# Two-layer attention trunk on one core: the general bias body, the rotary product and the casts of weight slices rewritten

## The chip, the cores and the metric

The kernel runs on one core of a Trainium2 chip. The metric is the device time of one execution in microseconds, the median of several runs. Engines are named as in the profile: PE is TensorE (matrix products; PEld its weight loads), DVE is VectorE, ACT is ScalarE, POOL is GpSimd, and SP is SyncE, which only issues transfers. ACT issues transfers too. Names with a q (ACTq, SPq) are an engine's instruction queue.

## What is computed

The input is x with 1024 rows of width 1024, and one integer position for each row. Two layers follow each other, each `h <- h + rmsnorm(mixer(rmsnorm(h)))`.

Layer A projects u = rmsnorm(x) to queries, keys, values and a gate (16 heads of 64). A row attends to its own chunk of 64 rows and the 8 chunks before. A learned bias per head is added to the scores, taken by the difference of positions clipped to -128..128:

```python
rel = jnp.clip(qpos[:, :, None] - kpos[:, None, :], -MAX_REL, MAX_REL) + MAX_REL
bias = jnp.take(rel_bias, rel, axis=1).transpose(1, 0, 2, 3)
```

After layer A one shared set of keys and values is projected from the residual stream. Layer B is differential attention on it: 8 heads with two softmax maps each, the second one subtracted with a learned factor, block-causal. Its queries and the shared keys get a rotary embedding on the first 16 of each 64 columns:

```python
return jnp.concatenate([t1 * cos - t2 * sin, t2 * cos + t1 * sin, t[..., ROT_DIM:]], axis=-1)
```

## The kernel before

All products are made in float32 in three passes: an operand is cut into a rounded part hi and a remainder lo (`hi_of`, line 188, a cast on ACT; `lo_of`, line 191, a subtraction on DVE), and hi·hi, hi·lo and lo·hi are added up (`mm_group`, line 264, lines 269, 271 and 273). A projection group is 24 matmuls into one of two accumulators, 512 rows at a time.

The order is written out by hand in ticks (class `Ticks`). In a tick PE issues four steps of the stream of dense products (`program`, line 1053), and each other piece of work is entered for a tick: `K.at` puts it ahead of the four, `K.after` and `K.later` behind them, `later(k)` k ticks from now, in the order of a rank and then of entry. Every engine works its own instructions strictly in the order in which they were issued. The stream is: 64 projection groups of layer A (head pairs u = 0 to 7; kinds key, query, value, gate; two halves of the rows), the output product of A, 64 groups of layer B, the output product of B. Attention steps of pair u are entered 24 ticks after its first group, one block of 128 rows every six ticks (`attA`, `attB`).

**The start.** Small loads, x tiles and the first weights are issued; ACT makes the square sums of x tiles 0 and 1 (`x_rstd`, line 355, its unused squares go to a slot of R2); PE makes 22 warm-up transposes. A flag tells whether the positions are not consecutive. It is read into a register of every engine (line 400), and `tc.If` (line 401) runs `general_bias` (line 1094), which builds the bias tiles for arbitrary positions. With the inputs here the flag is 0 and the body is jumped over. It holds 134 transfers on SP, unrolled over four groups of heads and eight row tiles, and inner loops. The pool `late` (line 404) is opened behind it and lies over its space; R1 and R2, which hold the operands of the dense products, lie elsewhere from the first. Then `norm_in` (line 475) normalises tile by tile (square sum on ACT, scale on POOL, line 480 on DVE), PE transposes (line 165), and ACT and DVE cut the result into R1.

**The bias.** For consecutive positions the bias tile of a head is the same for all rows. `bias_build` (line 441) makes it from a skewed copy of the table: `part1` loads it, `part2`, seven ticks later, fills its constant columns on DVE and stores it to slot 8 of the head's tensor `bias_t[h]`. `attA_pair` loads a tile for each block six ticks ahead of the scores, by an index that the flag selects (lines 635 to 637). `scores` (line 602) adds it on DVE and takes the maximum. The scores `sp` have a single buffer.

**Weight slices.** A's slices of 128x1024 are cut whole by `w_split` (line 199). B's are prepared during A (`Prepared.prepare`, line 230): loaded on ACT's queue, scaled on POOL (line 244), cut whole (`cut`, line 236), and stored by SP to `wcut` three ticks after the cast.

**The turn to layer B.** `layer_b_tiles` (line 869), six ticks ahead of B's first group, clears the cosine and sine tables, the mask and two buffers `sw` on POOL and loads the tables with eight transfers on SP.

**Rotation.** Each key or query group of B goes through `rope` (line 884). ACT copies the accumulator to `xs` (line 893); SP moves four strips of 8 rows into `sw` with rows swapped (lines 895, 896); DVE makes `xc`, the accumulator times the cosine (line 899); POOL multiplies `sw` by the sine (line 901) three ticks after the group; DVE adds both (line 902) six ticks after it, five for pair 0. A tick later ACT and DVE cut the sum into R1 (`split_k`, line 530, `split_q`, line 513); for a query, two transfers on SP (line 520, `R<-R`) copy the cut rows to the other half of the partitions. `xs`, `xc`, the values' copy `vt` and the gate's `th` share a ring of three buffers. In `attB_block` (line 922), `close` scales an output on DVE (line 1000) by a factor that POOL computes (lines 178, 179).

## Time and profile before

| | |
|---|---|
| median of 3 runs | 1328.13 us (1327.79 to 1331.78) |
| the profiled execution | 1329.67 us, span 1327.8 us |
| PE busy | 1290.0 us, 97% |
| DVE, ACT, POOL busy | 826.2, 685.1, 450.2 us |
| mean granted clock of PE | 0.99 |

The span runs from the first instruction to the last; the rest of an execution's time lies around it. A busy engine is not always one that sets the end: what counts is which engine waits for which, and when.

### The profile page before, as it was taken

The page shows a single profiled execution, that of the slowest core. Times are in us where ns is not written, and L with a number is a line of the kernel's source. Part 1 is how long each engine was busy: PE and PEld are TensorE (multiplying, and loading weights), DVE is VectorE, ACT ScalarE, POOL GpSimd, SP SyncE. Part 2 cuts the span into 40 slices and gives each one's busy share as a digit, 9 for nine tenths or more (in the row PEclk, how much of TensorE's full clock was granted, in tenths as well). Part 3 has the DMA queues.
Part 4 walks back from the last instruction along what each step waited for, and adds up shares of the span by engine and source line. Part 5 has one row for each costly group of instructions (what it writes and reads, how often), then busy time and mean ns, then how long its engine had stood idle before and what let it go on. Part 6 is the DMA issues. An engine that isn't in the chain of part 4 may idle for free.

```text
span 1327.8 us, 20645 instructions
## 1 busy us (share of the span) xinstructions
PE 1290.0 (97%) x6919; PEld 1090.8 (82%) x6919; DVE 826.2 (62%) x1719; ACT 685.1 (52%) x1488; POOL 450.2 (34%) x688
## 2 busy tenths in 40 slices
PE   6899999999999999999997999999999999999997
PEld 5788888888888888888886888888888888888786
DVE  5466665656575656665434676757575758588643
ACT  5456575656565656654333454545454545456311
POOL 1146444555545454442221222212121212122321
PEclk8999999999999999999998999999999999999999
DMA  5477767776677778655443232323232323225343
GB/s 215 117 259 226 229 216 233 242 233 231 229 251 246 236 223 268 205 176 151 148 134 115 77 107 73 107 76 108 75 109 74 109 74 109 74 78 172 99 151 107
DMA packets 103094, 211.24 MB, mean 159 GB/s; under 512 B 14432, under 2 KB 49280, under 8 KB 102976
## 3 DMA queue, kind: packets, MB, share of 16 engines
q1 hardware_dynamic: 80448, 135.85, 32.7%
q10 hardware_dynamic: 22528, 73.95, 17.2%
q8 instruction: 57, 0.93, 0.3%
q14 instruction: 61, 0.50, 0.1%
HBM read 135.19 MB, written 58.83 MB: 146 GB/s over the span
## 4 chain that ended last, share of the span: by engine, by line
PE 80%; issue 5%; POOL 5%; DVE 3%; ACT 2%; DMA 2%; SPq 1%; ACTq 0%; POOLq 0%; DVEq 0%
PE acc L269 15%; PE acc L271 14%; PE acc L273 14%; PE acc L782 12%; PE sp L597 8%; PE tp L165 8%; PE av L981 4%; PE av L699 4%; POOL st L169 1%; POOL s L651 1%; DVE R L192 1%; POOL w L244 1%; DMA skew<-rev 1%; ACT R L189 1%; DMA sw<-xs 0%
## 5 line engine op out<-in xcount | busy, mean ns | idle before, releaser
L273 PE MATMUL acc<-R,wlo 128*128 128x512 f32 x1008 | 410.4, 407 | 0.0
L269 PE MATMUL acc<-R,whi 128*128 128x512 f32 x1008 | 405.4, 402 | 0.7 <-DVE xc L899 0.7
L271 PE MATMUL acc<-R,whi 128*128 128x512 f32 x1008 | 404.7, 401 | 0.1
L612 ACT ACTIVATE s<-s,st 128x640 f32<-128x640 f32 (+7 forms) x256 | 188.2, 735 | 135.1 <-DVE st L606 131.5
L192 DVE TENSOR_TENSOR R<-tp,R 128x512 fp32r<-128x512 f32 (+3 forms) x304 | 178.8, 602 | 85.3 <-ACT R L189 83.9
L169 POOL TENSOR_TENSOR st<-st,mone 128x1 f32<-128x1 f32 x192 | 128.2, 668 | 277.5 <-ACT s L612 254.9
L273 PEld LDWEIGHTS acc<-R,wlo 128*128 128x128 f32 x1008 | 191.1, 190 | 33.0
L271 PEld LDWEIGHTS acc<-R,whi 128*128 128x128 f32 x1008 | 191.4, 190 | 30.8 <-DVE R L192 0.4
L269 PEld LDWEIGHTS acc<-R,whi 128*128 128x128 f32 x1008 | 191.7, 190 | 29.0 <-DVE xc L899 1.1
L189 ACT CAST R<-tp 128x512 fp32r<-128x512 f32 (+3 forms) x304 | 155.3, 515 | 107.6 <-PE tp L165 104.3
L597 PE MATMUL sp<-R 128*128 128x256 f32 (+3 forms) x768 | 174.3, 335 | 10.5 <-DVE st L606 6.3
L606 DVE CUSTOM_DVE_ANT_0 s<-sp,mask 128x256 f32<-128x256 f32 (+7 forms) x128 | 96.6, 755 | 111.3 <-PE sp L597 111.2
L597 PEld LDWEIGHTS sp<-R 128*128 128x128 f32 x768 | 136.4, 189 | 32.4 <-DVE st L606 8.1
L782 PE MATMUL acc<-R,ohi 128*128 128x512 f32 x512 | 161.0, 394 | 0.0
L606 DVE CUSTOM_DVE_ANT_0 s<-sp,bt 128x640 f32<-128x640 f32 (+4 forms) x128 | 83.7, 654 | 75.0 <-PE sp L597 50.0
L165 PEld LDWEIGHTS tp<-ident,s 128*128 128x128 f32 x768 | 96.0, 140 | 39.1 <-DVE s L950 10.6
L165 PE MATMUL tp<-ident,s 128*128 128x128 f32 x768 | 124.1, 274 | 0.9 <-DVE s L950 0.8
L901 POOL TENSOR_TENSOR sw<-sw,sin 128x512 f32<-128x512 f32 x32 | 43.0, 1344 | 225.0 <-DMA sw<-xs 203.9
L782 PEld LDWEIGHTS acc<-R,ohi 128*128 128x128 f32 x512 | 94.7, 188 | 18.5
L178 POOL TENSOR_SCALAR st<-st 128x1 f32<-128x1 f32 x80 | 20.7, 259 | 242.7 <-ACT tt L185 190.0
L782 PE MATMUL acc<-R,olo 128*128 128x512 f32 x256 | 101.5, 397 | 0.0
L651 POOL TENSOR_SCALAR s<-s,st 128x640 f32<-128x640 f32 (+4 forms) x128 | 90.7, 708 | 12.6
(123 smaller groups left out, 1639.2 us busy)
## 6 DMA issues: line engine op xcount, KB each, us to landing
bt<-bias_t SPq DMA_DIRECT2D x64, 320.0 KB
R<-R SPq DMA_DIRECT2D x64, 256.0 KB
wcut<-wh SPq DMA_DIRECT2D x32, 512.0 KB
wcut<-w SPq DMA_DIRECT2D x32, 512.0 KB
whi<-wcut ACTq DMA_DIRECT2D x32, 512.0 KB
wlo<-wcut ACTq DMA_DIRECT2D x32, 512.0 KB
wst<-in_a_w_in_dram ACTq DMA_DIRECT2D x29, 512.0 KB
w<-in_kv_w_dram ACTq DMA_DIRECT2D x16, 512.0 KB
```

The costliest lines, as they stand in the source:

```text
L165: T.transpose(dst, src, ident)
L169: G.tensor_tensor(out=r, in0=a, in1=mone, op=ALU.pow)
L189: A.copy(out=hi, in_=src)
L192: V.tensor_tensor(out=lo, in0=src, in1=hi.bitcast(F32), op=ALU.subtract)
L269: T.matmul(acc, lhsT=hi[:, c, :], rhs=xT(0, c), start=(c == 0), stop=False)
L271: T.matmul(acc, lhsT=hi[:, c, :], rhs=xT(1, c), start=False, stop=False)
L273: T.matmul(acc, lhsT=lo[:, c, :], rhs=xT(0, c), start=False, stop=(c == NC - 1))
L597: T.matmul(sp[:, a:b], lhsT=q[:, l, (i % 4) * P:(i % 4 + 1) * P], rhs=ks[:, head, j0 * P + a - c0:j0 * P + b - c0], start=(l == 0), stop=( ...
L606: V.tensor_tensor_reduce(out=s[:, 0:w], in0=sp, in1=add, op0=ALU.add, op1=ALU.min, scale=-0.125, scalar=BIG, accum_out=mx)
L612: A.activation(s[:, 0:w], s[:, 0:w], AF.Exp, bias=mx, scale=-1.0, accum_out=sums)
L651: G.tensor_scalar(out=s[:, 0:w], in0=s[:, 0:w], scalar1=r, scalar2=0.5, op0=ALU.mult, op1=ALU.mult)
L782: T.matmul(y, lhsT=lhs[:, c, :], rhs=R[:, n * 8 + c, l * 512:(l + 1) * 512], start=(m == 0), stop=(m == 23))
```

## The change

It has seven parts.

- `tc.If` gets `preferred_fallthrough_block=False`: the compiler is asked to place the code that follows when the flag is 0 right behind the branch.
- `general_bias` becomes a loop over the row tiles with all 16 heads at once and four transfers, on ACT's queue instead of SP's. For that the 16 tensors `bias_t[h]` become one tensor with the head as its first index.
- R1 and R2 move to a pool `resident` that is opened behind the general body and lies over its space; the pool `late` is opened ahead of it. The unused squares go to a tile `squares` in one of late's three `bb` buffers.
- `w_split` and `cut` cut a slice in two halves, a tick apart, and the store to `wcut` comes four ticks after the first cast instead of three.
- `part2` of the first two heads' bias comes four ticks after `part1` instead of seven.
- `layer_b_tiles` comes 40 ticks ahead of layer B instead of six.
- In `rope` the product with the cosine is made on POOL, in place in `xs`, two ticks after the group; DVE no longer reads the accumulator, and `xc` is gone. The sum is made six ticks after the group for pair 0 too, and in pair 0 the scores of blocks 0 and 1 are entered one tick later.

```diff
-    bias_t = [dp.tile([NT + 1, P, 640], F32, name=f"bias_t{h}") for h in range(AH)]
+    bias_t = dp.tile([AH, NT + 1, P, 640], F32, name="bias_t")
...
         hi, lo = w_tile("whi"), w_tile("wlo")
-        K.later(0, lambda: hi_of(w, hi), 2)
-        K.later(1, lambda: lo_of(w, hi, lo), 2)
+        for k in range(2):
+            c = slice(k * 4, k * 4 + 4)
+            K.later(k, lambda c=c: hi_of(w[:, c, :], hi[:, c, :]), 2)
+            K.later(k + 1, lambda c=c: lo_of(w[:, c, :], hi[:, c, :], lo[:, c, :]), 2)
...
-                K.later(0, lambda: hi_of(w, hi.bitcast(F32R)))
-                K.later(1, lambda: lo_of(w, hi.bitcast(F32R), w.bitcast(F32R)), 2)
-                K.later(3, lambda: [dma(out=wcut[k][:, 0, :], in_=hi), dma(out=wcut[k][:, 1, :], in_=w)])
+                for j in range(2):
+                    c = slice(j * 512, j * 512 + 512)
+                    K.later(j, lambda c=c: hi_of(w[:, c], hi[:, c].bitcast(F32R)), 2)
+                    K.later(j + 1, lambda c=c: lo_of(w[:, c], hi[:, c].bitcast(F32R), w[:, c].bitcast(F32R)), 2)
+                K.later(4, lambda: [dma(out=wcut[k][:, 0, :], in_=hi), dma(out=wcut[k][:, 1, :], in_=w)])
...
+    squares = lp.tile([P, D], F32, tag="bb", name="squares", bufs=3)
+
     def x_rstd(t):
-        return rstd_of([sumsq(xts[t], R2[:, 10 + t % 2, :])], D)
+        return rstd_of([sumsq(xts[t], squares)], D)
...
-    with tc.tile_pool(name="general", bufs=1) as gp, tc.If(flag > 0):
+
+    with tc.tile_pool(name="general", bufs=1) as gp, tc.If(flag > 0, preferred_fallthrough_block=False):
         general_bias(nc, tc, gp, positions, rel, bias_t)
-
-    lp = ctx.enter_context(tc.tile_pool(name="late", bufs=2))
+    rp = ctx.enter_context(tc.tile_pool(name="resident", bufs=1))
+    R1 = rp.tile([P, 16, 1024], F32R, name="R1")
+    R2 = rp.tile([P, 16, 1024], F32R, name="R2")
...
-            K.later(7, lambda: part2(b))
+            K.later(4 if h < 2 else 7, lambda: part2(b))
...
-            dma(out=bias_t[h][NT], in_=b[:, 0:640])
+            dma(out=bias_t[h, NT], in_=b[:, 0:640])
...
-                    in_=bias_t[2 * u + hh][bass.ds(flag * (i - NT) + NT, 1)]
+                    in_=bias_t[2 * u + hh, bass.ds(flag * (i - NT) + NT, 1)]
...
-    def rope(acc, half, first, then):
+    def rope(acc, half, then):
...
-        xc = lp.tile([P, 512], F32, tag="px", name="xc", bufs=3)
...
-        K.later(0, lambda: V.tensor_tensor(out=xc, in0=acc, in1=rot["cos"][:, cs], op=ALU.mult), 2)
-        k = 5 if first else 6
+        K.later(2, lambda: G.tensor_tensor(out=xs, in0=xs, in1=rot["cos"][:, cs], op=ALU.mult))
         K.later(3, lambda: G.tensor_tensor(out=w, in0=w, in1=rot["sin"][:, cs], op=ALU.mult))
-        K.later(k, lambda: V.tensor_tensor(out=xc, in0=xc, in1=w, op=ALU.add))
-        then(xc, k + 1)
+        K.later(6, lambda: V.tensor_tensor(out=xs, in0=xs, in1=w, op=ALU.add))
+        then(xs, 6 + 1)
...
-            attB_block(u, par, i, base + 6 * i + (max(0, 1 - i) if u == 0 else 0))
+            attB_block(u, par, i, base + 6 * i + (max(0, 2 - i) if u == 0 else 0))
...
-    K.after(start_b - 6, layer_b_tiles)
+    K.after(start_b - 40, layer_b_tiles)
...
 def general_bias(nc, tc, gp, positions, rel, bias_t):
...
-    dma = nc.sync.dma_start
+    dma = nc.scalar.dma_start
...
+    dma(out=tab, in_=rel.unsqueeze(0).broadcast_to([P, AH, NREL]))
...
-    for hg in range(0, AH, 4):
-        dma(out=tab, in_=rel[hg:hg + 4, :].unsqueeze(0).broadcast_to([P, 4, NREL]))
-        for i in range(NT):
...
+    with tc.For_i(0, NT, 1) as i:
...
+        with tc.For_i(0, NREL, 1) as t:
...
+            for h in range(AH):
+                V.scalar_tensor_tensor(out=acc[:, h, :], in0=msk, scalar=tab[:, h, bass.ds(t, 1)],
+                                       in1=acc[:, h, :], op0=ALU.mult, op1=ALU.add)
...
+        dma(out=bias_t[:, bass.ds(i, 1)].rearrange("h o p c -> (o p) h c"), in_=acc)
```

## Rows read from the trace of the kernel before

**Rows 1.** The page: span, and busy time of each engine.

```profile
span 1327.8 us, 20645 instructions
...
PE 1290.0 (97%) x6919; PEld 1090.8 (82%) x6919; DVE 826.2 (62%) x1719; ACT 685.1 (52%) x1488; POOL 450.2 (34%) x688
```

**Rows 2.** PE's waits, whole span: waited for, us in total, times, longest.

```profile
PE sp L597 <- DVE st L606: 6.3, 3, 4.7
...
PE sp L597 <- DMA R<-R: 4.1, 1, 4.1
PE av L699 <- DVE ot L719: 3.5, 3, 1.9
PE tp L165 <- ACT vt L548: 2.2, 1, 2.2
...
PE acc L269 <- DVE xc L899: 0.7, 1, 0.7
```

**Rows 3.** Line 401, the branch: ns min/median/max, first and last start in us.

```profile
L401 DVEq COMPARE_BRANCH  x1: 67/67/67, 7.7 to 7.7; - x1
...
L401 DVEq EVENT_SEMAPHORE  x1: 21/21/21, 13.4 to 13.4; - x1
```

**Rows 4.** DMA queues from 7 to 14 us: packets, MB, share.

```profile
q14 instruction: 5, 0.04, 1.7%
```

**Rows 5.** Timeline of the start: start us, us, instruction, [idle before <-releaser].

```profile
5.90 4.90 PE L165 MATMUL tp<-ident 128*128 128x128 f32 x22
...
10.29 0.55 POOL L179 TENSOR_TENSOR st<-st,mhalf 128x1 f32<-128x1 f32 x1
13.64 2.48 DVE L480 SCALAR_TENSOR_TENSOR xt<-xt,st,gbc 128x1024 f32<-128x1024 f32 x2 [6.40 <-DVEq L401]
```

**Rows 6.** The chain that ended last, 44 to 140 us: start us, us, what.

```profile
45.56 0.23 PE acc L271
...
46.06 3.52 DMA wst<-in_a_w_in_dram
...
54.63 4.05 DMA bt<-bias_t
```

**Rows 7.** Timelines of the turn, four engines, in order of time.

```profile
692.00 0.59 ACT L893 COPY xs<-acc 128x512 f32<-128x512 f32 x1
...
694.66 0.62 SPq L896 DMA_DIRECT2D sw<-xs  x1
...
696.77 1.30 POOL L901 TENSOR_TENSOR sw<-sw,sin 128x512 f32<-128x512 f32 x1 [6.81 <-DMA sw<-xs]
...
698.83 0.62 ACT L189 CAST R<-xc 64x512 fp32r<-64x512 f32 x1 [6.25 <-DVE xc L902]
...
700.12 0.59 ACT L893 COPY xs<-acc 128x512 f32<-128x512 f32 x1
...
703.52 1.15 SPq L520 DMA_DIRECT2D R<-R  x2
...
706.77 0.66 PE L597 MATMUL sp<-R 128*128 128x128 f32 x2 [4.10 <-DMA R<-R]
```

**Rows 8.** Windows: PE, PEld, DVE, ACT, POOL busy (instructions), PE clock, DMA.

```profile
59.00:65.00 6.00, 5.82 (x20) 4.71 (x21) 4.26 (x13) 2.13 (x8) 1.95 (x4) 0.72 0.55 142
705.00:725.00 20.00, 16.01 (x60) 12.81 (x61) 7.88 (x20) 6.92 (x17) 3.61 (x4) 0.76 0.45 131
740.00:1195.00 455.00, 454.93 (x2458) 382.27 (x2458) 311.17 (x733) 236.98 (x581) 108.30 (x190) 1.00 0.29 89
```

**Rows 9.** Groups by shape: count | busy us, mean ns | idle before.

```profile
L189 ACT CAST whi<-wst 128x1024 fp32r<-128x1024 f32 x32 | 33.4, 1045 | 7.2 <-issue 4.6 <-DMA lt<-in_b_lambda_k_dram 2.2
...
L899 DVE TENSOR_TENSOR xc<-acc,cos 128x512 f32<-128x512 f32 x32 | 22.1, 691 | 32.2 <-ACT xs L893 32.2
```

**Rows 10.** Line 901: ns min/median/max.

```profile
L901 POOL TENSOR_TENSOR sw<-sw,sin x32: 1261/1295/1590, 688.7 to 1185.8; 128x512 f32<-128x512 f32 x32
```

**Rows 11.** DVE's waits from 740 to 1195 us.

```profile
DVE s L606 <- PE sp L597: 98.2, 73, 2.3
```

More of the change, by code (lines that the diff above doesn't have):

```diff
@@ L325, in trunk @@
     adma(out=rr[:, 127:383], in_=rel[:, 0:256])
+    lp = ctx.enter_context(tc.tile_pool(name="late", bufs=2))
     xts = {}
@@ L912, in doneB @@
         elif kind == 1:
-            rope(acc, half, u == 0, lambda xs, k: split_q(xs, qqB, half, k))
+            rope(acc, half, lambda xs, k: split_q(xs, qqB, half, k))
         else:
@@ L1104, in general_bias @@
     idx = gp.tile([P, 640], F32, name="idx")
     msk = gp.tile([P, 640], F32, name="msk")
-    acc = gp.tile([P, 4, 640], F32, name="acc")
-    tab = gp.tile([P, 4, NREL], F32, name="tab")
     cnt = gp.tile([P, 1], F32, name="cnt")
+    acc = gp.tile([P, AH, 640], F32, name="acc")
+    tab = gp.tile([P, AH, NREL], F32, name="tab")
     dma(out=kk, in_=positions.broadcast_to([P, S]))
+    dma(out=tab, in_=rel.unsqueeze(0).broadcast_to([P, AH, NREL]))
+    dma(out=qi[:, 0:8], in_=positions.rearrange("o (i p) -> p (o i)", p=P))
@@ L1110, in general_bias @@
+    for k in (kh, kl):
+        V.memset(k[:, 0:512], 0.0)
     V.tensor_scalar(out=k2, in0=kk, scalar1=16, scalar2=None, op0=ALU.arith_shift_right)
-    V.tensor_copy(out=kh, in_=k2)
+    V.tensor_copy(out=kh[:, 512:512 + S], in_=k2)
     V.tensor_scalar(out=k2, in0=kk, scalar1=65535, scalar2=None, op0=ALU.bitwise_and)
-    V.tensor_copy(out=kl, in_=k2)
-    dma(out=qi[:, 0:8], in_=positions.rearrange("o (i p) -> p (o i)", p=P))
+    V.tensor_copy(out=kl[:, 512:512 + S], in_=k2)
     V.tensor_scalar(out=qi[:, 8:16], in0=qi[:, 0:8], scalar1=16, scalar2=None, op0=ALU.arith_shift_right)
```

48 lines of the change are left out of this document (19 added, 29 removed).

## The prediction

> **What bounds the kernel now.** I read the page first: TensorE is busy 1290.0 of 1327.8 us [rows 1]. No other engine exceeds 62%, so an edit can pay in two ways only: it removes one of TensorE's 38 idle microseconds, or it spares TensorE the stretch at the lower clock that follows a long idle. So I read what TensorE waited for [rows 2] and looked each wait up in time. The reader is to see three places.
>
> The start: VectorE executes the branch over the general body at 7.7 us and its next instruction comes at 13.4 [rows 3]. In that stretch an instruction queue fetches five packets of code between the data [rows 4], which I take for the far side of the branch. VectorE's first normalisation begins only at 13.64, although GpSimd had the first scale long before and the second by 10.84, and TensorE's warm-up transposes end at 10.80 [rows 5].
>
> The first scores: TensorE stands 4.7 us for VectorE [rows 2], because the bias tile comes late. The chain leads from a weight load issued at 46.06 through SyncE's small loads to the bias load at 54.63 [rows 6].
>
> The turn from layer A to layer B: 4.1 + 2.2 + 0.7 us of waits [rows 2]. The four rotary pieces of head pair 0 run one behind the other. Piece two is copied at 692.00, piece three only at 700.12, since ScalarE's casts of piece two stand ahead of it in the queue and wait 6.25 us for the rotation [rows 7]. A group of 24 matmuls at 0.23 us [rows 6] takes 5.5 us, so each piece falls 2.6 us further behind. In the rest of layer B TensorE is busy 454.93 of 455 us at full clock [rows 8]: nothing is to be had there, only lost.
>
> **The sum.** The profiled execution took 1329.67 us (span 1327.8), 1.5 us above the median 1328.13 of three. The terms are changes, so I take them off the median.
>
> Branch: with the false side next, the queue runs on. The floor is then the second normalisation, which can start at 10.84 instead of 13.64 + 2.48/2 = 14.88 [rows 5]: **4.0 us**. Bounds: 0 if the fetch stays, 5.7 if all of VectorE's pause counted [rows 3]. I take 4.0, as the warm-up ends at the same moment. The x loads for tiles 4 to 7, behind SyncE's branch, move ahead too. ScalarE's queue now carries the four transfers' bookkeeping; it has nothing to do between its second square sum and the first cast. The operand arrays lie over the general body's space, so their first writes wait for it; that body is skipped and VectorE passed it at 7.7.
>
> Turn: VectorE's 32 products from PSUM (0.69 us each [rows 9]) go, and so does their hold on the accumulator (the 0.7 us wait). GpSimd gets 32 products of 1.30 us [rows 10]. The first of a piece, two ticks after the copy, overwrites what the four transfers still read, so GpSimd's queue stops there for their landing, which it did a tick later before. The add stays at six ticks and moves from five for pair 0. That puts the casts a tick behind the next copy: ScalarE copies piece three when its group is done. For the query piece that TensorE waited for I count from its copy: 0.59, three issues of 0.62, 2.1 from the last issue to GpSimd's start, two products 2.6, the add 0.69, the cast 0.62, the remainder 0.69 (by the product of like size), 3.25 from the transfer's issue to TensorE's start [rows 7, 9]: 12.4 us. Without the 2.6 us that each piece fell behind, the copy starts at 689.4 and the piece is there at 701.8; TensorE waited from 706.77 - 4.10 = 702.67 on, 0.7 of which was the accumulator, and its scores now stand one tick (four matmuls, 0.9 us) later: about 702.9. The wait goes. At the lower clock TensorE did 16.01 us of work at 0.76 [rows 8]: 3.8 us lost. In all 7.0 + 3.8 = 10.8 could go. Late next is the fourth piece: ScalarE's casts of it still wait for two products, and the first mixed scores stand behind them. I leave 1.8 us for that: **9.0 us**, bounds 4 (the vt wait and its slow clock remain) and 10.8.
>
> Casts: 64 slices are cast in two pieces. A ScalarE cast is 1.045 us [rows 9], two halves by the 0.59 us copy [rows 7] are 1.18; 64 x 0.135 = 8.6 us more on ScalarE, and as much on VectorE, which both have idle. Gained is that an eviction waits behind half a cast. Layer A holds 1.6 us more of score waits and 3.5 of value waits [rows 2]. I take **1.5 us**, nearer to the gain since these waits are what half a cast shortens; bounds 5.1 gained, 3 lost (a third of the 8.6 reaching TensorE). The store, a tick later, has bias loads behind it in SyncE's queue, which are issued six ticks ahead of their use.
>
> At nothing: the earlier bias write (three ticks) is not what the bias load waits for [rows 6]; the earlier layer B tables fall behind a weight cast on GpSimd and before the next scale, and SyncE's eight small transfers there have an output slice behind them, loaded two groups (11 us) ahead; the one bias tensor could make a bias load wait for a write of another pair, some 2 us of landing, against a load issued six ticks ahead.
>
> 4.0 + 9.0 + 1.5 = 14.5: 1328.1 - 14.5 = **1313.6 us**.
>
> **Rivals.** A: the wait at the first scores goes as well. For: SyncE stood until the weight load landed (46.06 + 3.52 [rows 6]), though the two share no data, so it may be an accident of shared counters that another count of transfers undoes. Against: the eight small loads keep their place between the same neighbours. It gives 4.7 us and 5.82 x 0.28 = 1.6 of clock [rows 8]: 1307.3.
>
> B: the change doesn't do what it says: the compiler places the body next to the branch as before, or the code behind is not fetched in time. For: nothing in the trace shows where the code behind the branch will lie. Against: even out of order, a body this short leaves less to jump over. The 4.0 stay: 1317.6.
>
> C, slower: GpSimd's queue. In each later pair the rotary products end 1.30 us later; VectorE's sum of the rotation and its scaling of an output (line 1000), which needs a scale computed behind the products on GpSimd, stand 1.30 us longer, and the score reduction behind them frees the single score buffer later. If TensorE loses it whole in the 28 later pieces: 36 us, 1350. It decides from the point where the delay exceeds the pause that VectorE has ahead of a reduction: 98.2 us in 73 waits, 1.35 us each [rows 11]. That is as large as the delay, and VectorE no longer makes the 0.69 us product, so I give it little.
>
> [...]
>
> D: the fourth piece's delay at the turn is over 2 us and brings the slow clock back: half of the 9.0, 1318.
>
> **Chances.** Forecast 0.52 (its own range 1309 to 1318), A 0.24, B 0.10, D 0.07, C 0.03, E 0.01; 0.03 for B and D together with the casts' loss, which ends near 1325. A measurement tells about 0.3%, 4 us, from no change. Faster: 0.52 + 0.24 + 0.10 + 0.07 = 0.93; same 0.03; slower 0.03 + 0.01 = 0.04. The range 1304 to 1320 takes in A, B, D and the terms' bounds but not all of them at once.
>
> **What would show it.** Right: VectorE's first normalisation at about 8 us and its second near 10.9; TensorE's transposes of x near 11; in the turn no wait of 4 us on the query copy, copies 5.5 us apart, clock above 0.9; GpSimd with 64 products of 1.3 us. TensorE's busy time stays, its idle shrinks from 38 to under 28. [...]

## The result, and the profile after

The changed kernel takes 1311.92 us (median of 4 runs, 1311.60 to 1312.29); the kernel before, timed beside it again, 1329.56 (1327.79 to 1331.78). The ratio is 0.9867, with a 95% interval of 0.9848 to 0.9885. The forecast was 1313.6.

The total came out close to the forecast, but not by the terms of the sum. To see that, both traces are cut at the same events: the start of the eighth normalisation, of the fourth score reduction, of the last one of layer A, of the ninth and of the last one of layer B, and the end of the last product.

| stretch | before | after | gained | forecast |
|---|---|---|---|---|
| to the eighth normalisation | 35.77 | 31.20 | 4.6 | 4.0 |
| to the fourth score reduction (first scores) | 32.30 | 27.10 | 5.2 | 0 |
| to the last score reduction of layer A | 525.50 | 524.14 | 1.4 | 1.5 |
| to the ninth score reduction of layer B (turn) | 146.25 | 140.48 | 5.8 | 9.0 |
| to the last score reduction of layer B | 499.22 | 496.80 | 2.4 | 0 |
| to the last product (output product of B) | 82.01 | 83.23 | -1.2 | 0 |

Times in us; these are single executions. Two of the experiments below (b_part2_4 and b_arg) leave layer A, the turn, layer B and the output product of B as before: there these stretches took 524.3 and 523.9, 144.3 and 144.3, 499.3 and 499.3, 82.0 and 82.0 us. So layer A's gain is 0 to 1.4 and the turn's 3.8 to 5.8, while layer B and the output product repeat to a tenth. The starts of these two, 36.8 and 35.7, differ by 1. Part of such differences is the granted clock of TensorE. Its longest wait for `ot` in layer A is 1.9 to 2.3 us in every kernel here, between 181 and 193 us, and behind that wait the granted clock falls to 0.50 for a moment in some executions and not in others: in the kernel before it is 0.50 from 193 to 195 us and 0.66 as the mean from 192 to 197, 5 x 0.34 = 1.7 us lost, while the changed kernel has 1.00 from 182 to 187, behind the same wait. Why it falls in one and not in another is not shown.

The page of the changed kernel, first lines (answering to [rows 1]):

```profile
span 1309.8 us, 20786 instructions
...
PE 1283.2 (98%) x6919; PEld 1087.2 (83%) x6919; DVE 819.8 (63%) x1751; ACT 691.3 (53%) x1552; POOL 491.5 (38%) x720
```

TensorE's idle time went from 37.8 to 26.6 us, 11.2 less; its busy time went down as well, by 6.8. Three things add up in that: slow clock that is gone, short gaps that had counted as busy (layer B below), and, the other way, dense products that became slower (the place of the operands, below).

TensorE's waits over the whole span of the changed kernel (answering to [rows 2]):

```profile
PE av L706 <- DVE ot L726: 2.5, 2, 2.1
...
PE tp L163 <- DVE s L955: 2.4, 3, 1.7
PE sp L604 <- issue: 1.9, 1, 1.9
...
PE sp L604 <- DVE st L613: 1.0, 1, 1.0
```

The waits of 4.7 at the first scores, of 4.1 on the query copy, of 2.2 on `vt` and of 0.7 on `xc` are gone. New are 1.9 and 1.7 us at the turn. The line "issue" names no releaser; the timelines below do.

The start, VectorE's timeline of the changed kernel (answering to [rows 5]; there 13.64 and 2.48 for two):

```profile
8.48 1.28 DVE L487 SCALAR_TENSOR_TENSOR xt<-xt,st,gbc 128x1024 f32<-128x1024 f32 x1 [1.38 <-DVEq L407]
10.90 1.28 DVE L487 SCALAR_TENSOR_TENSOR xt<-xt,st,gbc 128x1024 f32<-128x1024 f32 x1 [1.13 <-POOL st L177]
```

The second normalisation stands where the prediction put it: it waits for its scale from GpSimd and starts at 10.90 instead of 14.88.

The first scores, SyncE's timeline (answering to [rows 6]):

```profile
39.52 0.58 SPq L428 DMA_DIRECT2D lt<-in_b_lambda_q_dram  x1
...
45.63 1.76 SPq L642 DMA_DIRECT2D bt<-bias_t  x3
```

Before, the first small load went out at 49.60, when the weight load had landed, and the bias load at 54.63. Now the small loads begin at 39.52, ahead of ScalarE's weight load, and the bias load follows at 45.63. This is rival A's mechanism.

The windows of the changed kernel (columns as in [rows 8]):

```profile
60.00:70.00 10.00, 10.00 (x52) 8.42 (x51) 4.37 (x11) 5.25 (x12) 5.06 (x8) 1.00 0.67 187
...
679.00:684.00 5.00, 5.00 (x23) 4.08 (x22) 2.07 (x3) 1.82 (x3) 2.00 (x2) 1.00 0.07 13
685.00:692.00 7.00, 7.00 (x32) 5.68 (x31) 2.06 (x3) 2.41 (x4) 1.94 (x2) 1.00 0.72 217
...
690.00:710.00 20.00, 16.31 (x78) 12.74 (x76) 8.90 (x25) 7.89 (x19) 6.12 (x6) 1.00 0.49 140
...
740.00:1180.00 440.00, 439.98 (x2394) 373.88 (x2393) 287.94 (x692) 231.11 (x571) 140.90 (x213) 1.00 0.29 90
```

The granted clock is 1.00 in all of them, also at the turn, where it was 0.76, although TensorE still idles 3.7 of the 20 us from 690 to 710. It is not so in every execution: in four kernels below with the same turn (a_noarg, a_operands_back, a_back_loop and a_casts_whole) the clock is 0.91 from 700 to 720 us, 20 x 0.09 = 1.8 us, and the turn takes 140.9 to 141.9 us. From 740 to 1180 TensorE is as busy as before.

The turn of the changed kernel, four engines in order of time (answering to [rows 7]):

```profile
679.61 0.59 ACT L899 COPY xs<-acc 128x512 f32<-128x512 f32 x1 [3.13 <-PE acc L275]
685.20 0.59 ACT L899 COPY xs<-acc 128x512 f32<-128x512 f32 x1 [2.17 <-PE acc L275]
687.87 0.62 SPq L902 DMA_DIRECT2D sw<-xs  x1
...
692.08 1.28 POOL L905 TENSOR_TENSOR xs<-xs,cos 128x512 f32<-128x512 f32 x1 [5.14 <-DMA sw<-xs]
...
694.64 0.69 DVE L907 TENSOR_TENSOR xs<-xs,sw 128x512 f32<-128x512 f32 x1 [4.89 <-POOL sw L906]
...
697.46 0.29 DVE L613 CUSTOM_DVE_ANT_0 s<-sp,mask 128x128 f32<-128x128 f32 x1
697.86 0.41 PE L604 MATMUL sp<-R 128*128 128x128 f32 x2 [1.94 <-issue]
...
705.33 0.30 PE L163 MATMUL tp<-ident,s 128*128 128x128 f32 x1 [1.68 <-DVE s L955]
```

The copies start when their group is done, 5.6 us apart, and not behind casts. Piece three (copied at 685.20) is where the new waits begin: its last strip is issued at 687.87, but GpSimd can start only at 692.08, 4.2 us later; for piece two of the kernel before that was 2.1 us [rows 7], and for piece four here it is 5.3 (693.65 to 698.93). The windows above show what else was on the way: from 685 to 692 the transfer engines are 72% taken, against 7% from 679 to 684, when piece two's strips moved. ScalarE issues the next weight slices in that time. That these make the strips late is argued from the windows; no run takes the slices away. VectorE's sum of piece three waits for GpSimd until 694.64, its remainders follow, and only then, at 697.46, does VectorE reduce the first scores, which TensorE had begun at 692.79. With the single score buffer the second scores wait: that is the 1.94 us.

### The profile page after: what moved, and what is told of

Read it like the earlier page. It is cut to its first block, busy times and chain, and to the rows that moved or that the text cites. A ratio compares the mean times of both kernels' runs of the same rounds, so it can differ in the third digit from the quotient of the medians.

```text
span 1309.8 us, 20786 instructions
## 1 busy us (share of the span) xinstructions
PE 1283.2 (98%) x6919; PEld 1087.2 (83%) x6919; DVE 819.8 (63%) x1751; ACT 691.3 (53%) x1552; POOL 491.5 (38%) x720
## 3 DMA queue, kind: packets, MB, share of 16 engines
HBM read 135.19 MB, written 58.83 MB: 148 GB/s over the span
## 4 chain that ended last, share of the span: by engine, by line
PE 91%; DVE 3%; ACT 2%; DMA 1%; issue 1%; POOL 1%; SPq 0%; ACTq 0%; DVEq 0%; POOLq 0%
PE acc L271 17%; PE acc L273 17%; PE acc L275 17%; PE acc L789 13%; PE tp L163 9%; PE sp L604 9%; PE av L706 5%; PE av L986 4%; DVE R L190 1%; DMA sw<-xs 1%; DMA wst<-in_a_w_in_dram 0%; PE acc L311 0%; DVE s L613 0%; ACT squares L183 0%; ACT R L187 0%
## 5 line engine op out<-in xcount | busy, mean ns | idle before, releaser
L167 POOL TENSOR_TENSOR st<-st,mone 128x1 f32<-128x1 f32 x192 | 116.3, 606 | 269.8 <-ACT s L619 256.5
L905 POOL TENSOR_TENSOR xs<-xs,cos 128x512 f32<-128x512 f32 x32 | 41.3, 1291 | 187.6 <-DMA sw<-xs 154.4
L658 POOL TENSOR_SCALAR s<-s,st 128x640 f32<-128x640 f32 (+4 forms) x128 | 100.5, 785 | 12.6
```

The lines of the kernel that those rows point to most:

```text
L167: G.tensor_tensor(out=r, in0=a, in1=mone, op=ALU.pow)
L658: G.tensor_scalar(out=s[:, 0:w], in0=s[:, 0:w], scalar1=r, scalar2=0.5, op0=ALU.mult, op1=ALU.mult)
```

## The experiments

All kernels were timed beside the kernel before, and of the stretches of the table the one that matters is given with each. The changed kernel itself was timed with the result alone, where the kernel before took 1329.56 us; beside the experiments it took 1327.5 to 1328.4. So whole times of an experiment and of the changed kernel that are less than some 3 us apart are not told apart, and there the stretches and the steps have to decide.

**The start: the argument or the length of the body.** First the argument alone, on the kernel before:

```diff
-    with tc.tile_pool(name="general", bufs=1) as gp, tc.If(flag > 0):
+    with tc.tile_pool(name="general", bufs=1) as gp, tc.If(flag > 0, preferred_fallthrough_block=False):
```

> The kernel before with only the argument that asks for the false side next to the branch; the general body keeps its 134 transfers. Theory 'argument': the far jump goes by the argument alone, VectorE's first normalisation starts near 8.5 us instead of 13.64, and the time falls by 4.0 to 4.6 us, to about 1325. Rival 'short body': what counts is how much code is jumped over; the argument alone leaves the five instruction packets and the 13.64, 1329.6 within 1 us.

Measured: 1328.47 against 1328.43 us, ratio 1.0003 (0.9993 to 1.0012): nothing. The branch line and VectorE's timeline:

```profile
L401 DVEq COMPARE_BRANCH  x2: 50/50/51, 7.6 to 7.8; - x2
```

```profile
13.41 2.48 DVE L480 SCALAR_TENSOR_TENSOR xt<-xt,st,gbc 128x1024 f32<-128x1024 f32 x2 [6.26 <-issue]
```

The argument does change the program: there are two branches instead of one. Behind the first the queue runs on at once, as the second starts 0.2 us later; the pause stands behind the second, from 7.8 to 13.41 us. The second is taken here for the jump over the body. Then the changed kernel with the argument taken out:

```diff
-    with tc.tile_pool(name="general", bufs=1) as gp, tc.If(flag > 0, preferred_fallthrough_block=False):
+    with tc.tile_pool(name="general", bufs=1) as gp, tc.If(flag > 0):
```

> The changed kernel without that argument, the body short as in the changed kernel. Theory 'argument': VectorE's first normalisation falls back from 8.48 to 13 us or more, and 4.0 to 4.6 us are lost: 1316.2. Rival 'short body': the first normalisation stays before 10 us and the time at 1311.9 within 1 us. Between the two: a fetch that is shorter because less code lies between, 1 to 3 us lost.

Measured: 1313.59 (1309.99 to 1314.15), ratio 0.9884 (0.9868 to 0.9900), within the spread of the changed kernel's 0.9867. The first normalisation starts at 8.35 us, the eighth at 31.10. So the short body gives the whole gain and the argument none that could be seen.

Two more kernels vary the body's length. Both have the operand arrays back in their first place, which leaves less room, so the body works on four heads at a time: once as four copies of its loop, once as one loop over the four groups.

```diff
+    R1 = cp.tile([P, 16, 1024], F32R, name="R1")
+    R2 = cp.tile([P, 16, 1024], F32R, name="R2")
...
-    with tc.For_i(0, NT, 1) as i:
+    for hg in range(0, AH, 4):
+        dma(out=tab, in_=rel[hg:hg + 4].unsqueeze(0).broadcast_to([P, 4, NREL]))
+        with tc.For_i(0, NT, 1) as i:
...
-    rp = ctx.enter_context(tc.tile_pool(name="resident", bufs=1))
-    R1 = rp.tile([P, 16, 1024], F32R, name="R1")
-    R2 = rp.tile([P, 16, 1024], F32R, name="R2")
+    lp = ctx.enter_context(tc.tile_pool(name="late", bufs=2))
```

> The changed kernel with the operand arrays R1 and R2 back in their first place and the pool of the late tiles behind the general body again; so that the body fits beside them it works on four heads at a time (four copies of its loop, ten transfers in place of four), and is jumped over as before. Theory 'place': the output products step at 0.233 to 0.236 us in the changed kernel against 0.229 to 0.233 before because the operands lie elsewhere; with the old place the steps are 0.229 to 0.233 again, 2.0 us less over the two output products: near 1310 if the start stays. Rival 'not the place': the steps stay at 0.233 to 0.236, and the time at 1311.9 within 1 us; the body of four loops can cost 0 to 2 us at the start in either case, which the first normalisation shows (8.5 us in the changed kernel).

Measured: 1312.58 us (1311.67 to 1312.94), ratio 0.9885 (0.9870 to 0.9900). And with one loop:

```diff
-    for hg in range(0, AH, 4):
-        dma(out=tab, in_=rel[hg:hg + 4].unsqueeze(0).broadcast_to([P, 4, NREL]))
+    with tc.For_i(0, AH // 4, 1) as g:
+        dma(out=tab, in_=rel[bass.ds(g * 4, 4)].unsqueeze(0).broadcast_to([P, 4, NREL]))
```

> The changed kernel with the operands in their first place and a body that is one loop over four groups of four heads (five transfers in the code; a_operands_back had four copies of the loop). Theory 'length of the body': the start's pause comes from the amount of code that is jumped over; with one loop the first normalisation is at 8.5 us again (13.5 in a_operands_back), while the steps stay at 236.0 and 229: start and place add up, 1312.6 - 4.9 = 1307.7, or 1311.9 - 5.4 = 1306.5. Rival 'place of the pools': the start was lost because the late tiles lie over the body's space again and their first writes wait for it; then the first normalisation stays at 13.5 and the time at 1312.6.

Measured: 1309.89 (1308.02 to 1311.30), ratio 0.9861 (0.9845 to 0.9877): 2 to 3 us over the 1306.5 to 1307.7 expected, for which see the place of the operands below. VectorE's first normalisation in a_operands_back, and in a_back_loop:

```profile
13.51 2.48 DVE L484 SCALAR_TENSOR_TENSOR xt<-xt,st,gbc 128x1024 f32<-128x1024 f32 x2 [6.45 <-issue]
```

```profile
8.57 1.28 DVE L484 SCALAR_TENSOR_TENSOR xt<-xt,st,gbc 128x1024 f32<-128x1024 f32 x1 [1.38 <-DVEq L406]
```

In both the late tiles lie over the body's space, so the rival on the pools falls: it is the length. In the built programs VectorE has 1512 instructions in the skipped part of the kernel before (pause), 276 in a_operands_back (pause), 100 in a_back_loop and 102 in the changed kernel (none). By what means the length makes the pause, these runs do not show. The instruction packets differ with it, though not those that the prediction read: the row beside them, which [rows 4] leaves out, is the one that changes with the pause. From 7 to 14 us, in the kernel before, in a_operands_back and in a_back_loop:

```profile
q8 instruction: 2, 0.03, 2.2%
```

```profile
q8 instruction: 1, 0.02, 0.9%
```

```profile
q14 instruction: 4, 0.03, 1.1%
```

The small packets of q14 are there with and without the pause. What comes with it is the larger packet on q8 (0.02 MB): the kernel before has two of them in this window, b_arg and a_operands_back one each, the changed kernel, a_noarg and a_back_loop none. Between 102 and 276 instructions nothing was measured.

**The first scores: one number.** The kernel before with the second stage of the first two biases four ticks after the first:

```diff
-            K.later(7, lambda: part2(b))
+            K.later(4 if h < 2 else 7, lambda: part2(b))
```

> The kernel before with one number of the change: the second stage of the first two heads' bias four ticks after the first instead of seven. Theory 'shared counter': the transfers report their end on a few counters that are dealt out when the program is built; this edit alone deals SyncE's first small load another counter than the weight load that ScalarE issues at 46.06. SyncE's wait of 5.6 us for that weight load goes, the first bias load is issued near 46 us instead of 54.63, TensorE's wait of 4.7 us at the first scores goes, the granted clock of 60 to 70 us rises from 0.86 to 1.00: 4.7 + 1.6 us less, near 1323.3 against 1329.6. Rival 'other parts': the wait went because of the four transfers in place of 134, the halved casts or the earlier start; then this edit, which I had put at nothing, changes less than 1 us and SyncE still waits for the weight load.

Measured: 1322.18 against 1328.43 us, ratio 0.9955 (0.9942 to 0.9969): 6.25 us from this number alone; 6.3 were expected. SyncE's wait in the kernel before, and SyncE's timeline and TensorE's window in b_part2_4:

```profile
SPq L421 <- DMA wst<-in_a_w_in_dram: 5.6, 1, 5.6
```

```profile
45.11 0.58 SPq L421 DMA_DIRECT2D lt<-in_b_lambda_q_dram  x1
...
52.09 1.53 SPq L635 DMA_DIRECT2D bt<-bias_t  x3
```

```profile
60.00:70.00 10.00, 10.00 (x53) 8.38 (x52) 3.03 (x9) 4.24 (x11) 4.62 (x9) 1.00 0.57 173
```

The wait for the weight load is gone, the clock of 60 to 70 us is 1.00 (0.86 before), and the stretch of the first scores takes 26.95 us like the changed kernel's 27.10. One detail was off: the bias load goes out at 52.09 and not near 46, since the eight small loads still take SyncE 7 us. That is only 2.5 us earlier than before, but the reduction that waits for it begins 4.0 us earlier (54.81 against 58.83), and TensorE comes to the first scores 2.2 us later (53.53 against 51.35), so that nothing is left of the wait of 4.7. The store of the bias itself was not what was late: it goes out at 39.32 here and at 41.64 before, both over 10 us ahead of the load. What the number moves is the order in which the eight counters of the built program are dealt. In the kernel before, the first small load is the next to use the counter of ScalarE's weight load and waits for that one to land (the 5.6 us above); with four ticks it is not, and goes out at 45.11 instead of 49.60. No data connects the two.

**The turn: ticks or product.** The changed kernel with the old ticks for pair 0, the product still on GpSimd:

```diff
-    def rope(acc, half, then):
+    def rope(acc, half, then, d=6):
...
-        K.later(6, lambda: V.tensor_tensor(out=xs, in0=xs, in1=w, op=ALU.add))
-        then(xs, 6 + 1)
+        K.later(d, lambda: V.tensor_tensor(out=xs, in0=xs, in1=w, op=ALU.add))
+        then(xs, d + 1)
...
-            attB_block(u, par, i, base + 6 * i + (max(0, 2 - i) if u == 0 else 0))
+            attB_block(u, par, i, base + 6 * i + (max(0, 1 - i) if u == 0 else 0))
```

(`d` is 5 for pair 0.)

> The changed kernel with the old ticks for head pair 0 of layer B: the sum of the rotation five ticks after the group instead of six, the scores of block 0 one tick later instead of two and one; the cosine product stays on GpSimd. Theory 'order of the casts': ScalarE's casts of a piece stand in front of its copy of the next piece again, so the copies are 8 us apart instead of 5.6, the wait of about 4 us on the query piece and the slow clock after it come back, and the time is 6 to 9 us longer: 1318 to 1321. Rival 'product': it was the shorter work on VectorE and the accumulator that is free earlier which closed the turn; then the ticks change less than 1.5 us: 1311 to 1313.

Measured: 1323.98 us (1323.00 to 1325.98), ratio 0.9972 (0.9962 to 0.9983): 12 us over the changed kernel, more than expected, and the stretch of the turn takes 152.25 us, 6 more than before the change. TensorE's waits, ScalarE's timeline and TensorE's window in a_ticks_old:

```profile
PE sp L604 <- DMA R<-R: 4.9, 1, 4.9
PE tp L163 <- ACT vt L555: 4.7, 1, 4.7
```

```profile
683.58 0.59 ACT L899 COPY xs<-acc 128x512 f32<-128x512 f32 x1
691.66 0.62 ACT L187 CAST R<-xs 64x512 fp32r<-64x512 f32 x1 [7.49 <-DVE xs L907]
...
692.94 0.59 ACT L899 COPY xs<-acc 128x512 f32<-128x512 f32 x1
```

```profile
690.00:710.00 20.00, 10.52 (x40) 7.73 (x38) 4.98 (x11) 4.62 (x10) 6.17 (x6) 0.83 0.45 139
```

ScalarE's casts stand ahead of the next copy again and wait 7.49 us; the copies are 9.4 us apart, against 8.2 before and 5.6 in the changed kernel. With the old order a slower product makes every piece slower, since each waits for the one ahead: GpSimd's second product of 1.3 us adds to every piece of the chain (the copies are 9.4 - 8.2 = 1.2 us further apart). So the turn is won by the one tick. What the move of the product does at the turn with the new ticks, the next kernel shows.

Then the product back on VectorE, with the new ticks:

```diff
+        xc = lp.tile([P, 512], F32, tag="px", name="xc", bufs=3)
...
-        K.later(2, lambda: G.tensor_tensor(out=xs, in0=xs, in1=rot["cos"][:, cs], op=ALU.mult))
+        K.later(0, lambda: V.tensor_tensor(out=xc, in0=acc, in1=rot["cos"][:, cs], op=ALU.mult), 2)
...
-        K.later(6, lambda: V.tensor_tensor(out=xs, in0=xs, in1=w, op=ALU.add))
+        K.later(6, lambda: V.tensor_tensor(out=xc, in0=xc, in1=w, op=ALU.add))
...
```

> The changed kernel with the cosine product back on VectorE, from the accumulator into a tile of its own; the ticks of the rotation stay as changed (sum at six ticks, scores of blocks 0 and 1 a tick later). Theory 'VectorE relieved': in layer B the mixed scores come late again by 0.13 to 0.17 us at three of eight blocks (steps from the last product to the transposes of 0.36, 0.38 and 0.40 us instead of 0.23), which is 3.4 us over layer B: 1315.3; the turn keeps its gain, since that comes from the order of the ticks. Rival 'GpSimd product makes the turn': ScalarE's casts come in front of the next copy again and the wait of 4 us on the query piece returns, 6 to 7 us more: 1318 to 1322. Rival 'neither': layer B's gain has another cause (the halved casts, the place of the operands) and the time stays within 1 us of 1311.9.

Measured: 1316.79 (1315.79 to 1318.45), ratio 0.9916 (0.9902 to 0.9929), 4.9 us over the changed kernel, 1.5 more than expected. In layer A the clock is 0.66 from 182 to 187 us, which is 1.7 of the 4.9. The turn takes 139.57 us against the changed kernel's 140.48, so the move to GpSimd is worth nothing there, and costs 0.9 if anything. With that all four combinations are measured: with the product on VectorE the new ticks bring the turn from 144.3 to 146.3 down to 139.57 us, with the product on GpSimd from 152.25 to 140.48. Layer B takes 501.46 instead of 496.80: 4.7 us. Here is one of the steps, TensorE's timeline of the changed kernel and of a_cos_dve:

```profile
751.69 0.40 PE L273 MATMUL acc<-R,whi 128*128 128x512 f32 x1
751.93 0.60 PE L163 MATMUL tp<-ident,s 128*128 128x128 f32 x4
```

```profile
752.88 0.40 PE L273 MATMUL acc<-R,whi 128*128 128x512 f32 x1
753.30 0.55 PE L163 MATMUL tp<-ident,s 128*128 128x128 f32 x3
```

From the last product to the transposes of the mixed scores it is 0.24 us in the one and 0.42 in the other. Between 740 and 1180 us there are 51 such steps in each kernel; their mean is 0.233 us in the changed kernel, 0.296 in a_cos_dve and 0.292 before. 51 x 0.063 is 3.2 us. The transposes behind them step at 0.109 us in the changed kernel and at 0.114 before, which is 1.1 more over 233 steps. None of it is listed as a wait: the profile counts TensorE as busy in a gap this short.

**The place of the operands.** a_operands_back, above, was also the test of this. In spite of its pause at the start (36.17 us to the eighth normalisation, 5.0 more than the changed kernel) its last product ends at 1302.70, against 1302.95. It gained 2.3 us in layer A, 2.0 in layer B and 1.2 in the output product of B. There the stream of TensorE holds nothing but dense products. Three of them make a period (two with `ohi`, one with `olo`); here are the `olo` products at both ends of eight periods, in the kernel before, in the changed kernel and in a_operands_padded (below):

```profile
1280.15 0.39 PE L782 MATMUL acc<-R,olo 128*128 128x512 f32 x1
...
1285.64 0.39 PE L782 MATMUL acc<-R,olo 128*128 128x512 f32 x1
```

```profile
1260.55 0.40 PE L789 MATMUL acc<-R,olo 128*128 128x512 f32 x1
...
1266.15 0.40 PE L789 MATMUL acc<-R,olo 128*128 128x512 f32 x1
```

```profile
1259.62 0.39 PE L790 MATMUL acc<-R,olo 128*128 128x512 f32 x1
...
1265.11 0.39 PE L790 MATMUL acc<-R,olo 128*128 128x512 f32 x1
```

24 steps take 5.49, 5.60 and 5.49 us: 228.8, 233.3 and 228.8 ns each, at the same granted clock of 1.00. The same shows in layer A, where the first of the three products of a projection steps at 236.0, 237.8 and 236.0 ns (means of the steps under 0.3 us). In the built programs R1 begins at byte 1152 of its partition before, at 97728 after; R2, which the output product of B reads, lies 65536 bytes further on in both. The third kernel only moves it by 192 bytes:

```diff
     rp = ctx.enter_context(tc.tile_pool(name="resident", bufs=1))
+    pad = rp.tile([P, 48], F32, name="pad")
     R1 = rp.tile([P, 16, 1024], F32R, name="R1")
```

> The changed kernel with 192 bytes of unused space ahead of R1 in each partition, so that R1 and R2 stand 192 bytes further up; nothing else. With the operands back in their first place every dense product of 512 columns stepped 1 to 4 ns faster (layer A, first of three products: 236.0 ns against 237.8; output product of B: 228.9 against 233.3), some 5 us in all. Theory 'alignment': R1 began at byte 1152, which is 128 over a multiple of 512, and in the changed kernel at 97728, 448 over; the padding makes it 97920, again 128 over, and the steps come back to 236.0 and 229: 5 us less, 1307. Rival 'region': what counts is which part of the partition the operands fill, or how they lie to the weights at 24384 to 48960; 192 bytes change nothing there, the steps stay at 237.8 and 233.3 and the time at 1311.9 within 1 us.

Measured: 1308.38 us (four runs between 1305.67 and 1310.79), ratio 0.9860 (0.9841 to 0.9879). The four runs fall into two near 1306, at a mean granted clock of 0.997 and 0.998, and two near 1310.6, at 0.995; 0.0025 of 1305 us are 3.3. The profiled execution is one of the first two: span 1303.9 us against 1309.8. The whole times alone would not show the gain, since the intervals of the ratios cover each other; the steps do. 192 unused bytes bring back the old steps everywhere. That decides for the alignment and against the region.

a_back_loop has the old steps too (230.0 ns in layer A where a step follows without a break, like the kernel before; 232.0 in the changed kernel), but in its profiled execution, the slowest of its four, layer A (524.81 us) and layer B (497.22) took no less than in the changed kernel. Its clock is 0.66 from 224 to 229 us, 1.7 us, and TensorE idles 1.1 us more in layer A and 1.2 in layer B; without these it is where a_operands_padded is. So the steps are worth 5 to 6 us between executions without such losses, and 2.0 to 3.5 by the medians.

Which alignment, the next kernel was to tell. It has 64 bytes instead of 192, and a new edit of the ticks with it (a_late_half, below):

```diff
+    pad = rp.tile([P, 16], F32, name="pad")
```

> The two gains together: the sums of pieces three and four nine ticks after the group, as in a_late_half, and ahead of R1 64 bytes of unused space instead of 192, so that the operands begin at byte 97792, a multiple of 512. Theory 'multiple of 128': 192 bytes helped because they took R1 from a multiple of 64 to a multiple of 128 (1152 and 97920 are such, 97728 is not); then 64 bytes do the same, the dense steps are 236.0 and 229 ns, and the gains add up: 1311.9 - 3.5 to 5.9 - 2.8 = 1303.2 to 1305.6. Rival 'same residue': R1 has to lie 128 bytes over a multiple of 256 or 512, as in the kernel before; then the steps stay at 237.8 and 233.3 or take a third value, and only the 2.8 us of the ticks are left: 1309.1.

Measured: 1313.21 (1312.57 to 1315.18), ratio 0.9897 (0.9880 to 0.9913). TensorE's timeline in it, as above:

```profile
1261.81 0.39 PE L790 MATMUL acc<-R,olo 128*128 128x512 f32 x1
...
1267.41 0.39 PE L790 MATMUL acc<-R,olo 128*128 128x512 f32 x1
```

5.60 us again, 233.3 ns; in layer A the first products step at 238.6. "A multiple of 128" falls: R1 at 97792 is a multiple of 512 and is as slow as at 97728. The two fast places, 1152 and 97920, both lie 128 bytes over a multiple of 256 and of 512. Whether that is what counts, and whether the place of the weights counts with it, these runs leave open. The kernel also fell short of its own rival's 1309.1: its layer A took 527.90 us, 3.8 over the changed kernel. The slower steps explain about 1, and 1.7 the clock, which is 0.66 from 182 to 187 us. The turn took 137.35 us, as in a_late_half below.

**What is left of the turn.** A new edit on the changed kernel. For pair 0 the sums of pieces three and four come nine ticks after the group:

```diff
-            rope(acc, half, lambda xs, k: split_q(xs, qqB, half, k))
+            rope(acc, half, lambda xs, k: split_q(xs, qqB, half, k), 9 if (u, half) == (0, 1) else 6)
```

(The same for the key, and `rope` takes the number of ticks as `d`, as above.)

> The changed kernel with one new edit: for the second half of the rows of head pair 0 in layer B (pieces three and four) the sum of the rotation comes nine ticks after the group instead of six. Theory 'VectorE's queue': TensorE's two waits left in the turn (1.94 us at the second scores, 1.68 us at the first mixed scores) stand for VectorE's sums and remainders of pieces three and four, which wait for GpSimd in front of the score reductions; three ticks later the reductions come first and 3 to 3.6 us go: 1308.5. Rival 'late pieces': blocks 4 and 5, which read these pieces, then wait, or the ring of three tiles holds up the copy of the values; the time is the same or up to 3 us longer.

Measured: 1309.15 us (1307.68 to 1309.17), ratio 0.9855 (0.9840 to 0.9870), 2.8 us under the changed kernel, which alone would not be clear; the turn takes 137.25 us instead of 140.48. TensorE's waits and window:

```profile
PE sp L604 <- DMA R<-R: 0.9, 1, 0.9
PE tp L163 <- DVE s L955: 0.8, 2, 0.6
```

```profile
690.00:710.00 20.00, 19.09 (x93) 15.56 (x92) 10.36 (x30) 9.22 (x23) 6.24 (x6) 1.00 0.49 141
```

VectorE reduces the first scores at 694.25, ahead of the sum of piece three, and TensorE's idle time from 690 to 710 us goes from 3.7 to 0.9. The waits stood for VectorE's queue.

**Whole casts, and late tables.** The changed kernel with whole slices:

```diff
-        for k in range(2):
-            c = slice(k * 4, k * 4 + 4)
-            K.later(k, lambda c=c: hi_of(w[:, c, :], hi[:, c, :]), 2)
-            K.later(k + 1, lambda c=c: lo_of(w[:, c, :], hi[:, c, :], lo[:, c, :]), 2)
+        K.later(0, lambda: hi_of(w, hi), 2)
+        K.later(1, lambda: lo_of(w, hi, lo), 2)
```

(and `cut` with its store likewise)

> The changed kernel with the slices of the weights cut whole again and stored three ticks after the cast. Theory 'halves gain': the gain of layer A behind the first scores (9.7 us ahead at 71 us, 11.1 at 608) came from evictions that wait behind half a cast; it goes, 1.4 us, and TensorE's waits for values and scores are 1 to 2 us longer: 1313.4. Rival 'no effect': these waits come from elsewhere and the time stays within 0.7 us of 1311.9. Rival 'halves cost': the two fixed costs per cast reached TensorE, and whole casts are 1 to 3 us faster: 1309 to 1311.

Measured: 1315.61 us (1311.25 to 1317.65), ratio 0.9903 (0.9885 to 0.9920). TensorE's waits in it:

```profile
PE av L702 <- DVE ot L722: 3.4, 3, 1.9
...
PE sp L600 <- DVE st L609: 1.5, 2, 1.1
```

```profile
182.00:187.00 5.00, 4.33 (x16) 3.85 (x17) 3.45 (x8) 4.02 (x9) 3.55 (x5) 0.66 0.51 135
```

The waits were 2.5 and 1.0 in the changed kernel: 1.4 us, the size that was expected, and the halves do gain. The kernels agree: the wait for `ot` is 3.4 to 3.8 us in three pieces in the four kernels with whole casts and 2.4 to 2.5 in two in the ten with halves. The whole difference is 3.7 us, with a spread of the runs as wide as itself. In the profiled execution layer A took 3.2 us longer; the 1.7 that are left are the clock of the window above, which falls so in a_cos_dve and a_pad64_late too, whose casts are halved. At the turn the clock is 0.91 from 700 to 720 us, as in a_noarg. So 1.4 is shown for the casts, more is not.

Last, the tables of layer B six ticks ahead again:

```diff
-    K.after(start_b - 40, layer_b_tiles)
+    K.after(start_b - 6, layer_b_tiles)
```

> The changed kernel with the cosine and sine tables of layer B six ticks ahead of its first group again, as before. Theory 'at nothing', as in the prediction: the clearing on GpSimd and the eight small transfers stand in nobody's way at either place; the time stays within 1.5 us of 1311.9 and the first rotation is as far behind its copy as in the changed kernel (5.2 us). Rival 'cover': the transfers on SyncE and the clearing on GpSimd late in layer A delay the first rotation pieces or the output slices, and the time is 2 to 4 us longer.

Measured: 1312.24 us (1311.88 to 1312.63), ratio 0.9887 (0.9870 to 0.9903). GpSimd's first product comes 5.2 us after its copy (675.23 and 680.41), the same as in the changed kernel. The place of the tables is worth nothing that could be seen.

## Why the prediction was right in the time, and where its steps failed

**The start (4.0 forecast, 4.6 gained).** The size and the floor were right: the second normalisation at 10.90 sets it. The step that failed is "with the false side next, the queue runs on". The argument did nothing; the length of the body did all. Rival B's reserve, that "a body this short leaves less to jump over", is what the runs bear out. The packets of [rows 4] were no sign of it, as such packets are there without the pause too (four in a_back_loop).

**The first scores (0 forecast, 5.2 gained).** Rival A happened. The step that failed stood under "at nothing": that the earlier bias write is not what the bias load waits for. That is true of the data, and yet this edit alone gave 6.25 us, because it changes which transfers share a counter. The price in rival A (4.7 + 1.6) was right, its cause nearly so: not the number of transfers but the order in which they are dealt.

**The turn (9.0 forecast, 3.8 to 5.8 gained).** The mechanism was right: copies as soon as the groups are done, 5.6 us apart (5.5 forecast), no wait on the query copy, the clock at 1.00. The term that was mis-sized is what is "late next". 1.8 us were left for the fourth piece; it was pieces three and four, and they cost 1.9 + 1.7 in waits. Rival D is not far off: the clock held in this execution, but is 0.91 behind these waits in a_noarg, whose turn is the same. The working took 2.1 us from the last issue to GpSimd's start, by piece two of before [rows 7]; for piece three it was 4.2 and for piece four 5.3. And it counted the delay only on the piece's own way: what TensorE waited for was the score reductions that stood behind these pieces in VectorE's queue.

**The casts (1.5 forecast, about 1.4 shown).** Right in size, by the same two waits that the prediction named. That the table's 1.4 for layer A is the same number is chance: it holds this gain, 1.7 us of slow clock in the kernel before, and what the slower products took away.

**Layer B ("nothing is to be had there, only lost"; 2.4 gained).** The step that failed is reading "454.93 of 455" [rows 8] as full. VectorE's relief closed gaps of 0.13 to 0.17 us in three of eight blocks, worth 4.7 us by a_cos_dve. Rival C's fear, that GpSimd's products delay VectorE there, did not show: the products took 1277 to 1302 and 1282 to 1312 ns, and TensorE waited for no reduction there. Nor did a loss from GpSimd's products running beside VectorE's work (E in the chances), but the changed kernel hardly puts it to the test: no product in it runs beside a sum or remainder of the rotation for more than 0.01 us. The kernel before does. Of its 32 products [rows 10] six lasted 1543 to 1590 ns and the other 26 at most 1305. The six are those that began beside a remainder `R<-xc,R` of VectorE; here is one pair, the second of the two remainders beginning at 760.50:

```profile
759.77 1.41 DVE L192 TENSOR_TENSOR R<-xc,R 64x512 fp32r<-64x512 f32 x2
760.75 1.59 POOL L901 TENSOR_TENSOR sw<-sw,sin 128x512 f32<-128x512 f32 x1 [6.01 <-DMA sw<-xs]
```

Beside each other for 0.39 to 0.43 us, the products took 0.25 to 0.30 us more than their median of 1295 ns and the remainders kept their 687; the eight products that ran beside a remainder `R<-tp,R` took 1284 to 1305 ns. b_part2_4 and a_cos_dve have six pairs of the first kind each, with products of 1514 to 1583 ns. So what was longer in such a pair was GpSimd's product, behind VectorE's instruction that came first; a pair in which GpSimd came first no run shows.

**The operands' place (0 forecast, 5 to 6 lost).** The prediction asked only whether their first writes wait. That the pace of the dense products goes with the address (228.8 or 233.3 ns a step in the output product of B) was in no step; like the gaps of layer B it lies outside the "two ways only" in which the working let an edit pay. It took 1.2 us in the output product of B, where it stands bare, and by a_operands_padded 2.0 in layer A, up to 1.5 at the turn and 0.9 in layer B; the medians show 3.5 of the sum and those of a_back_loop 2.0. It hid 2 us of what layer A gained otherwise.

So the time was near by luck, for a sum of errors that cancel. Against the table's forecasts they are +0.6, +5.2, -0.1, -3.2, +2.4 and -1.2 us, together +3.7: 18.1 us of span gained where 14.5 were forecast. 1.4 of that vanish in the figure, since the forecast was made against 1328.13 and the kernel before took 1329.56 beside the changed one.

## What to carry to other kernels

When a small edit moves transfers about, look at which wait of a queue has no data behind it: an issue that waits for a transfer of another tile may share its counter, and a change of order removed 6 us here. When large arrays move, compare the step from one dense product to the next in the stream, to a nanosecond, before and after; an offset of 192 bytes was worth more here (5.9 us between two executions without slow clock, 3.5 by the medians) than the halved casts or the tables. A piece of work that is moved to a slower engine pays only if the order of the queues lets it run beside the next piece; with one tick less the same kernel was 12 us slower. Two edits go beyond the changed kernel by their own stretches, the 192 bytes and the nine ticks (the turn 3.2 us shorter); by the whole times, 3.5 and 2.8 us, neither is clear of the noise, and they were not run together.

## What the runs showed that was not expected

- The step from one 512-column float32 product to the next, in the output product of B at a granted clock of 1.00, went with the start byte of the operand arrays: 228.8 ns with R1 at byte 1152 of a partition (the kernel before) or 97920 (a_operands_padded), 233.3 at 97728 (the changed kernel) or 97792 (a_pad64_late).
- TensorE counted as busy hides gaps: 51 steps of 0.292 us instead of 0.233 were part of 454.93 busy microseconds out of 455.
- The branch over skipped code cost about 5 us or nothing by its length: VectorE's first normalisation starts at 13.51 us with 276 of VectorE's instructions in between (a_operands_back), at 8.48 with 102 (the changed kernel).
- GpSimd's rotary product lasted 1.54 to 1.59 us instead of 1.30 when it began beside VectorE's subtraction `R<-xc,R`: six of 32 in the kernel before, none in the changed kernel.
